# A decoder trunk on one core: the second rotary matmul of the attention scores on 128 rows where it took 64

## The chip, the cores and the metric

The kernel runs on one core of one Trainium2 chip. The metric is the device time of one execution in microseconds (us). Its engines run side by side and each takes its own instructions in order: TensorE (PE in the profile; PEld is its weight-load port), VectorE (DVE), ScalarE (ACT), GpSimd (POOL) and SyncE (SP), which issues the transfers. TensorE multiplies a stationary tile, loaded first, with a moving tile that streams through it; the sums collect in banks of PSUM.

## What is computed

The reference is a trunk of two layers on 512 tokens with 1024 channels: an HGRN2 recurrence in the first, latent attention (MLA) with 16 heads in the second, each with feed-forward half steps around it, and a gated embedding per layer. The change lies in the scores of the attention, which are the sum of a part without position (128 channels) and a rotary part (64 channels) whose key all heads share:

```python
s = (jnp.einsum('bqhd,bkhd->bhqk', qn, k_nope)
     + jnp.einsum('bqhd,bkd->bhqk', qr, k_rope)).astype(jnp.float32) * scale
...
s = jnp.where(mask[None, None], s, -jnp.inf)
pr = jax.nn.softmax(s, axis=-1).astype(v.dtype)
return jnp.einsum('bhqk,bkhd->bqhd', pr, v)
```

## The kernel before

Activations lie with channels on the 128 partitions and the 512 tokens along the row. Weights are one stream of 128x128 blocks in the order of use; a fetch brings eight of them (`raw`), ScalarE rounds them to a high half (`whi`, L125) and VectorE subtracts to get the low half (`wlo`, L126). Every float32 product is made of three matmuls on such halves: high by high, high by low and low by high (`mm3`, L142 to L144). `split` (L157, L158) makes the halves of an activation.

The instructions of an engine are put in order once, when the program is built, by a scheduler that works from the dependences and its own estimate of times. So TensorE's queue in the attention interleaves the scores of one head, the transposes and the weighting of the head before it, and the projections, and the order does not change at run time.

The attention is `mla`. For each head `scores` makes four blocks of 128 queries; block i has keys 0 to 128 (i + 1), so its matmuls stream 128, 256, 384 or 512 columns. A block takes five matmuls into one bank of the tag `aux`: the three of `mm3` for the channels without position, then two for the rotary part, L774 and L775. The tile `qr` of a head holds the 64 rotary channels twice: `rope` copies the high halves to partitions 0 to 63 and the low halves to 64 to 127. The key `krope` also holds its 64 channels twice, on partitions 0 to 63 and again on 64 to 127, because it comes out of a matmul with a constant that adds up pairs and repeats them; `krope[0]` is its high half and `krope[1]` its low half, both on 128 partitions.

L774 multiplies all 128 rows of `qr` with `krope[0]`: high by high and low by high at once. L775 multiplies rows 0 to 63 of `qr` with rows 0 to 63 of `krope[1]`: high by low. It ends the accumulation of the block. Behind it VectorE adds the mask and takes the maximum (L779, L783), ScalarE takes the exponential (L786), VectorE the reciprocal of the sum (L788) and GpSimd scales (L789). In `weigh` TensorE transposes the probabilities (L800), ScalarE and VectorE split them (`ph` L804, `pl` L805), and TensorE multiplies with the values.

In the first layer `recur` has other matmuls on a part of the array: at L440 it takes stationary tiles of 64 columns and writes 64 partitions.

Of the kernel before, what the change touches and what calls it, by code (L numbers as in the profile page):

```python
# [54 lines left out]
def kernel(  # L55
# [12 lines left out]
    act, dve, pool, pe = nc.scalar, nc.vector, nc.gpsimd, nc.tensor  # L68
# [14 lines left out]
    def slot(s="s", dt=F32, tag="s"):  # L83
        return spool.tile([P, T], dt, tag=tag, bufs=BUFS[tag], name=name(s))

    def tiny(n=4):
        return tpool.tile([P, n], F32, tag="t", bufs=40, name=name("t"))
# [4 lines left out]
    def aux_bank():  # L92
        return psum.tile([P, T], F32, tag="aux", bufs=4, name=name("aux"))
# [2 lines left out]
    FETCH_OFF = 200  # L96
    EV_OFF = 400

# [1 line left out]
    vc = cpool.tile([P, V_N], F32, name="vc")  # L100
    cs = cpool.tile([P, C_N], F32, name="cs")
    ident = cs[:, C_ID : C_ID + P]
# [3 lines left out]
    dve.memset(ones, 1.0)  # L106
    jmat = cs[:, C_J : C_J + P]

# [1 line left out]
    stream = {"n": 0, "tiles": 0, "ready": [], "now": None}  # L110

    def soon(n):
# [28 lines left out]
    def mm3(out, a, b, first, last):  # L141
        pe.matmul(out, a[0], b[0], start=first, stop=False)  # L142
        pe.matmul(out, a[0], b[1], start=False, stop=False)  # L143
        pe.matmul(out, a[1], b[0], start=False, stop=last)  # L144

    def chain(rhs):
        ps = mm_bank()
        n = len(rhs)
        for k in range(n):
            mm3(ps, block(), rhs[k], k == 0, k == n - 1)  # L150
        return ps

# [1 line left out]
    def split(src, scale=None, tag="s"):  # L154
        hi, lo = slot("hi", F32R, tag), slot("lo", F32R, tag)
        if scale is None:
            act.copy(hi, src)  # L157
            dve.tensor_tensor(out=lo, in0=src, in1=hi.bitcast(F32), op=ALU.subtract)  # L158
        else:
            act.activation(hi, src, AF.Copy, scale=scale)  # L160
            dve.scalar_tensor_tensor(  # L161
                out=lo, in0=src, scalar=scale, in1=hi.bitcast(F32), op0=ALU.mult, op1=ALU.subtract
            )
        return hi, lo

# [1 line left out]
    class Stats:  # L167
        def __init__(self, n):
            self.n, self.acc, self.seen = n, None, 0
# [50 lines left out]
        act.copy(rb, pb)  # L220
        return r, rb

# [1 line left out]
    x = [slot("x") for _ in range(KC)]  # L224

    def load(c):
# [2 lines left out]
    def gain(col, c):  # L229
        return vc[:, col + c : col + c + 1]  # L230

# [1 line left out]
    def ffn(xg, rb, post, beside=None, primed=()):  # L233
        primed = list(primed)
        for half in range(2):
            hidden = []
            for f in range(NH):
                pg, pu = (primed.pop(0) if primed else chain(xg) for _ in range(2))
                g = slot("g", F32, "r")
                dve.tensor_tensor(out=g, in0=pg, in1=rb, op=ALU.mult)  # L240
                act.activation(g, g, AF.Silu)  # L241
                pool.tensor_tensor(out=g, in0=g, in1=rb, op=ALU.mult)  # L242
                dve.tensor_tensor(out=g, in0=pu, in1=g, op=ALU.mult)  # L243
                hidden.append(split(g, None, "o" if f < 4 else "v" if f < 8 else "s"))
                if half == 1 and f == 5 and beside is not None:
                    beside()
            for m in range(KC):
                po = chain(hidden)
                dve.scalar_tensor_tensor(  # L249
                    out=x[m], in0=po, scalar=0.5, in1=x[m], op0=ALU.mult, op1=ALU.add  # L250
                )
                if half == 1:
                    post(m)
# [12 lines left out]
    def gcol(layer, i):  # L266
        return V_GAIN + (layer * 4 + i) * KC

# [1 line left out]
    def bounds():  # L270
        lbt = tpool.tile([P, 6 * A_HEADS], F32, tag="lb", bufs=1, name="lbt")
        lg0 = vc[:, V_LB : V_LB + A_HEADS]
        lg1 = vc[:, V_LB + A_HEADS : V_LB + 2 * A_HEADS]
        part = [lbt[:, i * A_HEADS : (i + 1) * A_HEADS] for i in range(6)]
        dve.tensor_tensor(out=part[0], in0=lg0, in1=lg1, op=ALU.max)
        dve.tensor_tensor(out=part[1], in0=lg0, in1=part[0], op=ALU.subtract)
        dve.tensor_tensor(out=part[2], in0=lg1, in1=part[0], op=ALU.subtract)
        act.activation(lbt[:, 3 * A_HEADS : 5 * A_HEADS], lbt[:, A_HEADS : 3 * A_HEADS], AF.Exp)
        dve.tensor_tensor(out=part[5], in0=part[3], in1=part[4], op=ALU.add)
        dve.reciprocal(part[0], part[5])  # L280
        dve.tensor_tensor(out=part[1], in0=part[3], in1=part[0], op=ALU.mult)
        dve.tensor_scalar(out=part[2], in0=part[1], scalar1=-1.0, scalar2=1.0, op0=ALU.mult, op1=ALU.add)
        return part[1], part[2]

# [1 line left out]
    def hgrn(xg, stats, lower, upper, post):  # L286
        rt, rb = rows(stats)
        mk = slot("mk", I32)
# [243 lines left out]
                    finish(2 * p + e, *res[e], sg[e])  # L532
        project(1)

# [1 line left out]
    def embed(layer):  # L536
        pp = []
        for c in range(2):
            raw = slot("p", F32, "r")
            nc.scalar.dma_start(raw, pT[layer, c * P : (c + 1) * P, :])  # L540
            pp.append(split(raw, None, "p"))
        return pp
# [15 lines left out]
            post(m)  # L558
        return emb

# [1 line left out]
    def last(xg, pp, rb):  # L562
        scaled, stats, halves = [], Stats(KC - 1), []

# [46 lines left out]
                        dve.tensor_tensor(out=o[:, c], in0=scaled[n][:, s], in1=r, op=ALU.mult)  # L611
                nc.sync.dma_start(view[i], o)

# [1 line left out]
    def rotary():  # L615
        pi_ = slot("pos", I32, "r")
        nc.scalar.dma_start(pi_, pos.to_broadcast([P, T]))
# [34 lines left out]
        act.activation(cos, rq, AF.Sin)  # L652
        return sin, cos

# [1 line left out]
    class Shared:  # L656
        def __init__(self):
            self.banks = [aux_bank() for _ in range(3)]
# [41 lines left out]
            cn.append(split(c))  # L700
        return cn, krope

# [1 line left out]
    def mla(xg, stats, cn, krope, sin, cos, post):  # L704
        _, rb = rows(stats)
        st = Stats(4)
# [33 lines left out]
        def values(p):  # L740
            w = [block(2) for _ in range(2)]
            tiles = []
            for i in range(2):
                pv = mm_bank()
                for n in range(2):
                    j = 2 * i + n
                    for k in range(2):
                        ck = tuple(a[:, j * P : (j + 1) * P] for a in cn[k])
                        mm3(pv[:, 256 * n : 256 * n + 256], ck, w[k], k == 0, k == 1)
                tiles.append(split(pv, None, "v"))  # L750
            return [
                [
                    tuple(a[:, 256 * (j % 2) + P * e : 256 * (j % 2) + P * e + P] for a in tiles[j // 2])
                    for j in range(NT)
                ]
                for e in range(2)
            ]

        def scores(qr):
            pk = chain(cn)  # L760
            kk = split(pk)
            pq = chain(cq)
            qq = split(pq)
            pt = [slot("P", F32, "r") for _ in range(3)]
            where = [(1, 384), (2, 0), (1, 0), (0, 0)]
            den = tiny()
            res = []
            for i in range(NT):
                w = (i + 1) * P
                qs = slice(i * P, w)  # L770
                ps = aux_bank()
                s = ps[:, 0:w]
                mm3(s, (qq[0][:, qs], qq[1][:, qs]), (kk[0][:, 0:w], kk[1][:, 0:w]), True, False)
                pe.matmul(s, qr[:, qs], krope[0][:, 0:w], start=False, stop=False)  # L774
                pe.matmul(s, qr[0:64, qs], krope[1][0:64, 0:w], start=False, stop=True)  # L775
                b, o = where[i]
                p = pt[b][:, o : o + w]
                mx, nb = tiny(1), tiny(1)
                dve.tensor_tensor_reduce(  # L779
                    out=p, in0=s, in1=cs[:, C_MASK + T - w : C_MASK + T], scale=1.0, scalar=-3.0e38,  # L780
                    op0=ALU.add, op1=ALU.max, accum_out=mx,
                )
                dve.tensor_scalar(  # L783
                    out=nb, in0=mx, scalar1=sc[:, i : i + 1], scalar2=-1.0, op0=ALU.mult, op1=ALU.mult
                )
                act.activation(p, p, AF.Exp, bias=nb, scale=sc[:, i : i + 1], accum_out=den[:, i : i + 1])  # L786
                rl = tiny(1)
                dve.reciprocal(rl, den[:, i : i + 1])  # L788
                pool.tensor_scalar(out=p, in0=p, scalar1=rl, scalar2=1.0, op0=ALU.mult, op1=ALU.mult)  # L789
                res.append(p)  # L790
            return res
# [34 lines left out]
        qr, vals = rope(0), values(0)  # L826
        last = None
        for h in range(B_HEADS):
            ahead = h < B_HEADS - 1
            rotated, value = qr[h % 4], vals[h % 2]  # L830
            if h % 4 == 3 and ahead:
                qr = rope(h // 4 + 1)
# [5 lines left out]
            last = (pr, value)  # L838
# [4 lines left out]
        for part in range(2):  # L843
            project(B_HEADS // 2 - 1, part)

# [1 line left out]
    first = Next([gcol(0, 0)])  # L847
    primed, heads = [mm_bank() for _ in range(4)], []

# [40 lines left out]
    tables, held = [], []  # L890
# [7 lines left out]
    sin, cos, lower, upper = tables  # L898
# [18 lines left out]
    cn, krope = shared(sh, sin, cos)  # L917
# [168 lines left out]
```

## Time and profile before

| | us |
|---|---|
| median of three runs | 2247.5 |
| lowest and highest run | 2247.43, 2249.44 |
| profiled execution: span, first to last instruction | 2245.4 |
| TensorE matmuls busy in the span | 2223.7 |
| VectorE busy | 1160.0 |
| ScalarE busy | 775.0 |
| GpSimd busy | 422.8 |

The profile gives the span of the profiled execution, and no other time of it. The matmuls of L775 start between 1513.3 and 1788.1 us of the span, all within the attention. In the timeline a row has the start, the time of the instruction, the engine, the line, the operation, what is written from what is read (the moving tile first, then the stationary one), the rows and columns of the array that are in use (128*128 is the whole array, 64*128 the upper half of its rows) and the moving tile's size. The time of a matmul overlaps with the next one's, so what a matmul takes of the queue is read from one start to the next.

### The profile page before, as it was taken

What the parts mean: (1) busy time and instruction counts of PE and PEld (TensorE: products, weight loads), DVE (VectorE), ACT (ScalarE), POOL (GpSimd) and SP (SyncE); (2) the same over time, 40 slices, a digit from 0 to 9 for tenths busy, and PEclk for the clock granted to TensorE, in tenths of its full rate; (3) what the DMA queues carried; (4) which work ended last, traced back from release to release, by engine and by line L of the source; (5) the groups of instructions that cost most, each with busy time, mean ns of one, the idle gap of its engine ahead of it and who ended that gap; (6) DMA issues with size and microseconds to landing.
All of it is one profiled execution on the core that took longest, in us unless ns stands there. A gap on an engine that the chain in (4) does not pass through costs nothing.

```text
span 2245.4 us, 26413 instructions
## 1 busy us (share of the span) xinstructions
PE 2223.7 (99%) x10434; PEld 1847.4 (82%) x10434; DVE 1160.0 (52%) x1798; ACT 775.0 (35%) x1125; POOL 422.8 (19%) x441
## 2 busy tenths in 40 slices
PE   8999999999999999999999999999999999999998
PEld 6888888899888888888888888887878788888887
DVE  5433544778875433445654344466666664334345
ACT  4322333223343222334432132345444442223244
POOL 2100111555431101111111011112111121001111
PEclk9999999999999999999999999999999999999999
DMA  4333332222223333332333333332223123333332
GB/s 163 98 94 98 104 94 90 83 67 66 67 66 103 96 101 94 105 102 89 99 94 94 103 95 94 101 95 77 62 71 94 38 85 94 97 101 103 99 99 66
DMA packets 60523, 204.42 MB, mean 91 GB/s; under 512 B 7408, under 2 KB 9584, under 8 KB 60400
## 3 DMA queue, kind: packets, MB, share of 16 engines
q1 hardware_dynamic: 59536, 201.28, 29.3%
q8 instruction: 82, 1.34, 0.3%
q10 hardware_dynamic: 864, 1.46, 0.2%
q14 instruction: 41, 0.34, 0.0%
HBM read 196.42 MB, written 2.10 MB: 88 GB/s over the span
## 4 chain that ended last, share of the span: by engine, by line
PE 98%; DVE 1%; ACT 0%; issue 0%; DMA 0%; POOL 0%; SPq 0%; DVEq 0%; ACTq 0%
PE mm L142 29%; PE mm L143 29%; PE mm L144 29%; PE aux L144 1%; PE aux L143 1%; PE aux L396 1%; PE aux L142 1%; PE aux L775 1%; PE aux L800 1%; PE aux L774 0%; PE aux L205 0%; PE aux L213 0%; PE aux L196 0%; PE aux L440 0%; DVE o L611 0%
## 5 line engine op out<-in xcount | busy, mean ns | idle before, releaser
L142 PE MATMUL mm<-hi,whi 128*128 128x512 f32 x2824 | 1097.2, 391 | 8.5 <-ACT whi L125 6.2
L143 PE MATMUL mm<-lo,whi 128*128 128x512 f32 x2824 | 1103.6, 391 | 2.0 <-DVE lo L161 2.0
L144 PE MATMUL mm<-hi,wlo 128*128 128x512 f32 x2824 | 1101.0, 390 | 0.0
L125 ACT CAST whi<-raw 128x1024 fp32r<-128x1024 f32 (+2 forms) x372 | 386.5, 1041 | 1101.0 <-PE mm L143 792.0
L142 PEld LDWEIGHTS mm<-hi,whi 128*128 128x128 f32 x2824 | 530.1, 188 | 119.8 <-ACT whi L125 6.2
L143 PEld LDWEIGHTS mm<-lo,whi 128*128 128x128 f32 x2824 | 530.8, 188 | 111.5 <-DVE lo L161 4.1
L144 PEld LDWEIGHTS mm<-hi,wlo 128*128 128x128 f32 x2824 | 530.8, 188 | 110.0 <-issue 0.9
L126 DVE TENSOR_TENSOR wlo<-raw,whi 128x1024 fp32r<-128x1024 f32 (+2 forms) x372 | 463.9, 1248 | 273.2 <-ACT whi L125 253.5
L242 POOL TENSOR_TENSOR g<-g,rb 128x512 f32<-128x512 f32 x88 | 152.0, 1729 | 984.3 <-ACT g L241 984.3
L243 DVE TENSOR_TENSOR g<-mm,g 128x512 f32<-128x512 f32 x88 | 60.9, 691 | 262.7 <-PE mm L144 254.1
L240 DVE TENSOR_TENSOR g<-mm,rb 128x512 f32<-128x512 f32 x88 | 60.4, 691 | 205.9 <-PE mm L144 205.9
L179 POOL TENSOR_TENSOR sq<-sq,sq 128x512 f32<-128x512 f32 x55 | 80.6, 1465 | 334.9 <-ACT sq L174 334.1
L249 DVE SCALAR_TENSOR_TENSOR x<-mm,x 128x512 f32<-128x512 f32 x64 | 44.2, 691 | 106.7 <-PE mm L144 105.6
L789 POOL TENSOR_SCALAR P<-P,t 128x128 f32<-128x128 f32 (+1 forms) x64 | 35.3, 551 | 243.7 <-DVE t L788 207.3
L160 ACT ACTIVATE hi<-x,vc 128x512 fp32r<-128x512 f32 x72 | 51.4, 718 | 77.4 <-DVE x L249 57.3
L161 DVE SCALAR_TENSOR_TENSOR lo<-x,vc,hi 128x512 fp32r<-128x512 f32 x72 | 63.1, 884 | 25.5 <-ACT hi L160 25.4
L158 DVE TENSOR_TENSOR lo<-g,hi 128x512 fp32r<-128x512 f32 x88 | 60.1, 685 | 0.9 <-ACT hi L157 0.7
L786 ACT ACTIVATE P<-P,t,t 128x128 f32<-128x128 f32 (+1 forms) x64 | 42.0, 656 | 53.6 <-DVE t L783 53.3
L822 DVE TENSOR_TENSOR x<-mm,x 128x512 f32<-128x512 f32 x64 | 43.7, 687 | 26.0 <-PE mm L144 25.6
L157 ACT CAST hi<-g 128x512 fp32r<-128x512 f32 x88 | 54.5, 621 | 6.8 <-DVE g L243 6.8
L241 ACT ACTIVATE g<-g 128x512 f32<-128x512 f32 x88 | 55.0, 628 | 1.8 <-DVE g L240 1.2
L142 PE MATMUL mm<-whi,hi 128*128 128x256 f32 x192 | 55.2, 288 | 0.0
(199 smaller groups left out, 1596.6 us busy)
## 6 DMA issues: line engine op xcount, KB each, us to landing
raw<-in_wall SPq DMA_DIRECT2D x367, 512.0 KB, 3.5
x<-in_xT SPq DMA_DIRECT2D x8, 256.0 KB, 5.8
qr<-hi SPq DMA_DIRECT2D x32, 64.0 KB, 2.0
qr<-lo SPq DMA_DIRECT2D x32, 64.0 KB, 2.0
out_dram<-o SPq DMA_DIRECT2D x8, 256.0 KB, 2.5
p<-in_pT ACTq DMA_DIRECT2D x4, 256.0 KB, 2.8
cs<-in_cst SPq DMA_DIRECT2D x1, 385.0 KB, 7.2
pos<-in_pos ACTq DMA_DIRECT2D x1, 256.0 KB, 3.2
```

The lines of the kernel that those rows point to most:

```text
L125: act.copy(hi[:, s], raw[:, s])
L126: dve.tensor_tensor(out=lo[:, s], in0=raw[:, s], in1=hi[:, s].bitcast(F32), op=ALU.subtract)
L142: pe.matmul(out, a[0], b[0], start=first, stop=False)
L143: pe.matmul(out, a[0], b[1], start=False, stop=False)
L144: pe.matmul(out, a[1], b[0], start=False, stop=last)
L158: dve.tensor_tensor(out=lo, in0=src, in1=hi.bitcast(F32), op=ALU.subtract)
L161: dve.scalar_tensor_tensor(out=lo, in0=src, scalar=scale, in1=hi.bitcast(F32), op0=ALU.mult, op1=ALU.subtract)
L179: eng.tensor_tensor(out=self.acc, in0=self.acc, in1=sq, op=ALU.add)
L240: dve.tensor_tensor(out=g, in0=pg, in1=rb, op=ALU.mult)
L241: act.activation(g, g, AF.Silu)
L242: pool.tensor_tensor(out=g, in0=g, in1=rb, op=ALU.mult)
L243: dve.tensor_tensor(out=g, in0=pu, in1=g, op=ALU.mult)
```

## The change

The second rotary matmul takes all 128 partitions of both operands. It thereby adds the product of the low halves of queries and keys, which lie on partitions 64 to 127, to the same sum. The number of instructions, their order on all five engines, their buffers and their waits are the same; in the program the size of the array's part at L775 is 128 by 128 where it was 64 by 128. Elsewhere the diff only takes comments out.

```diff
@@ scores, in mla @@
                 mm3(s, (qq[0][:, qs], qq[1][:, qs]), (kk[0][:, 0:w], kk[1][:, 0:w]), True, False)
                 pe.matmul(s, qr[:, qs], krope[0][:, 0:w], start=False, stop=False)
-                pe.matmul(s, qr[0:64, qs], krope[1][0:64, 0:w], start=False, stop=True)
+                pe.matmul(s, qr[:, qs], krope[1][:, 0:w], start=False, stop=True)
```

## Rows read from the trace of the kernel before

**Rows 1.** The page: the span, and the chain that ended last by engine.

```profile
span 2245.4 us, 26413 instructions
...
PE 98%; DVE 1%; ACT 0%; issue 0%; DMA 0%; POOL 0%; SPq 0%; DVEq 0%; ACTq 0%
```

**Rows 2.** Windows, attention stretch: its length, busy us of each engine (instructions), clock.

```profile
1510.00:1790.00 280.00, 277.88 (x1396) 222.31 (x1395) 184.79 (x450) 132.53 (x266) 42.61 (x69) 1.00 0.24 71
```

**Rows 3.** Both rotary lines: weight loads, min/median/max ns, first and last start.

```profile
L774 PEld LDWEIGHTS aux<-hi,qr x64: 186/188/192, 1513.0 to 1787.6; 128*128 128x128 f32 x64
...
L775 PEld LDWEIGHTS aux<-lo,qr x64: 182/183/183, 1513.3 to 1788.1; 64*128 64x128 f32 x64
```

**Rows 4.** Timeline of TensorE's matmuls around one block of 512 columns.

```profile
1526.14 0.39 PE L142 MATMUL aux<-hi,hi 128*128 128x512 f32 x1
...
1526.59 0.39 PE L144 MATMUL aux<-hi,lo 128*128 128x512 f32 x1
1526.82 0.39 PE L774 MATMUL aux<-hi,qr 128*128 128x512 f32 x1
1527.13 0.50 PE L775 MATMUL aux<-lo,qr 64*128 64x512 f32 x1
1527.56 0.50 PE L144 MATMUL mm<-hi,wlo 128*128 128x512 f32 x1
1527.90 0.39 PE L142 MATMUL mm<-hi,whi 128*128 128x512 f32 x1
```

**Rows 5.** Timeline of the load port there; in brackets the idle time before.

```profile
1527.13 0.18 PEld L775 LDWEIGHTS aux<-lo,qr 64*128 64x128 f32 x1 [0.35 <-issue]
1527.56 0.19 PEld L144 LDWEIGHTS mm<-hi,wlo 128*128 128x128 f32 x1 [0.25 <-issue]
```

**Rows 6.** Timeline of TensorE's matmuls, one head's blocks of 128, 256, 384 columns.

```profile
1536.27 0.27 PE L144 MATMUL aux<-ph,lo 128*128 128x128 f32 x1
1536.38 0.28 PE L774 MATMUL aux<-hi,qr 128*128 128x128 f32 x1
...
1536.83 0.38 PE L142 MATMUL aux<-hi,hi 128*128 128x256 f32 x1
1537.06 0.28 PE L143 MATMUL aux<-lo,hi 128*128 128x256 f32 x1
...
1537.29 0.28 PE L774 MATMUL aux<-hi,qr 128*128 128x256 f32 x1
...
1537.81 0.44 PE L142 MATMUL aux<-hi,hi 128*128 128x384 f32 x1
1538.09 0.34 PE L143 MATMUL aux<-lo,hi 128*128 128x384 f32 x1
...
1538.44 0.34 PE L774 MATMUL aux<-hi,qr 128*128 128x384 f32 x1
...
1539.08 0.50 PE L143 MATMUL mm<-lo,whi 128*128 128x512 f32 x1
1539.42 0.40 PE L144 MATMUL mm<-hi,wlo 128*128 128x512 f32 x1
```

**Rows 7.** Timeline around two groups of L440, first layer: exit, then entry.

```profile
435.81 0.50 PE L144 MATMUL mm<-hi,wlo 128*128 128x512 f32 x1
436.15 0.39 PE L142 MATMUL mm<-hi,whi 128*128 128x512 f32 x1
...
440.71 0.39 PE L144 MATMUL mm<-hi,wlo 128*128 128x512 f32 x1
441.03 0.68 PE L440 MATMUL aux<-qq,k 128*64 128x64 f32 x8
```

**Rows 8.** Waits of TensorE's matmuls in 1510 to 1790: us, times, longest.

```profile
PE aux L143 <- DVE pl L805: 1.1, 3, 0.5
PE aux L144 <- DVE lo L158: 0.5, 1, 0.5
PE aux L142 <- ACT ph L804: 0.2, 1, 0.2
```

## Prediction

> **What bounds the kernel now.** I read the views from the outside in. First the page: the chain of work that ended last is TensorE's own for 98% of a span of 2245.4 us [rows 1], so a microsecond taken out of TensorE's queue is a microsecond of the kernel unless a wait takes its place. Then the windows view of the stretch in which all 64 executions of the changed line fall, 1510 to 1790 us [rows 2]: TensorE's matmuls are busy 277.88 of 280.00 us there, VectorE 184.79, ScalarE 132.53, and the granted clock is 1.00, the upper of its two levels (2.4 GHz). TensorE is the bound of this stretch with much room beside it. Busy time does not tell what a matmul costs, though, because matmuls overlap; the cost is the distance from one start to the next. So the third view is the timeline of TensorE around the changed line (L775), and the reader should subtract neighbouring starts.
>
> **The steady pitch.** Between full-array matmuls of the same width the starts lie 0.227 us apart at 512 columns (three steps from 1526.14 to 1526.82 cover 0.68) [rows 4], 0.175 at 384 (two steps from 1538.09 to 1538.44), 0.12 at 256 (two steps from 1537.06 to 1537.29, 0.115 before rounding up) and 0.11 at 128 (1536.27 to 1536.38) [rows 6]. The full-array first rotary matmul (L774) sits in this pitch: it starts one pitch behind its predecessor.
>
> **What the half-array matmul costs today.** In the same block L775 starts 0.31 us behind L774, not 0.227; the matmul behind it starts 0.43 later (1527.13 to 1527.56), and the one after that 0.34 later (1527.56 to 1527.90) [rows 4]. Only then is the pitch back. The weight loads show why: L775's load begins after 0.35 us in which the load port waited for nothing that the profile shows, and the next full-array load again after 0.25 us [rows 5]. Both loads begin at the very time at which their own matmul is put down as started (1527.13 and 1527.56 in both views) [rows 4, 5], so no matmul ahead hides them: neither on the way into the half array nor on the way out. The cost is therefore not in the 64 rows but in two changes of the array's shape.
>
> A second place in the trace agrees, with another shape: the 64-column matmuls of the first layer (L440, 128*64). Going in, the first one starts 0.32 us behind a 512-wide full-array matmul (440.71 to 441.03); coming out, the second full-array matmul starts 0.34 us behind the first (435.81 to 436.15) [rows 7]. These are the same two numbers, 0.31 and 0.34, at a place that shares neither tile nor line with the attention. What the two places share is the change of shape.
>
> **What the change removes.** It adds no instruction and moves none: on all five engines the order is the same. L774, just ahead, already reads all 128 rows of the same query tile, so no transfer is waited for that was not waited for before. The 64 matmuls of L775 (one for each of the 64 loads of [rows 3]) become what L774 is: the same stationary tile, a moving tile of the same kind and width. I cost each at one pitch of its width and let the two shape changes go. From the start of L774, over three steps (L774, L775, the one behind), I take today's distance less three pitches:
> - 512 columns: 1526.82 to 1527.90 is 1.08 us, less 3 x 0.227 = 0.68, leaves 0.40 [rows 4].
> - 384 columns, followed by 512: 1538.44 to 1539.42 is 0.98, less 0.175 + 0.175 + 0.227 = 0.58, leaves 0.40 [rows 6].
> - 256 columns, followed by 384: 1537.29 to 1538.09 is 0.80, less 0.12 + 0.12 + 0.175 = 0.415, leaves 0.385 [rows 6].
> - 128 columns, followed by 256: 1536.38 to 1537.06 is 0.68, less 0.11 + 0.11 + 0.12 = 0.34, leaves 0.34 [rows 6].
>
> One head has one of each: 0.40 + 0.40 + 0.385 + 0.34 = 1.525 us. There are 16 heads, and the blocks that follow each other directly share no step, so nothing is counted twice: 16 x 1.525 = 24.4 us. The rows allow some 0.2 us more or less (rounding of hundredths). The upper end is about 1.3 us higher: a wide load behind a narrow full-array matmul can be hidden partly in the work ahead, and 16 such places at up to 0.08 us (0.11 less 0.03, if the narrow matmul cost next to nothing) give that. So 25.7 us is the most.
>
> **What can be given back.** TensorE arrives earlier at each wait behind the scores. The waits that it has in this stretch are few: 1.1 us in three places for the low half of the probabilities (L805), 0.5 in one for a low half (L158), 0.2 in one for a high half (L804) [rows 8]. At each of these five places the wait could grow by what TensorE has gained since the last one. If that is a whole head's gain each time, 5 x 1.525 = 7.6 us are lost; that is the lower end, a gain of 16.8. If nothing is lost, zero. I take 1 us, close to zero, because the chain that is waited for at the L805 and L804 places starts with the transposes of the probabilities on TensorE itself, behind the scores: it starts earlier by as much as its reader does. What is not started by TensorE, the splitting of weights, runs on engines that are idle for 95 us (VectorE) and 147 us (ScalarE) of the 280 [rows 2]; shortening the stretch by 24 us leaves both well below TensorE.
>
> **Sum.** 24.4 less 1.0 is 23.4 us. Against the profiled execution: 2245.4 - 23.4 = 2222.0 us of span. The median of the runs, 2247.5, stands 2.1 us above that span; I carry these over: 2224.1 us, a ratio of 0.990.
>
> **Rivals.**
> *The rows do not matter (same time).* The mechanism: a matmul and its load take what their columns take, and the excess around L775 belongs to something that stays, such as the end of the accumulation in that bank or the same query tile being loaded twice. The result is 2247.5 us. For it: the loads are as long, 183 ns at 64 rows and 188 at 128 [rows 3]. Against it: the last matmul of an accumulation in another bank (L144 at 1536.27, the end of the weighting) has its successor one pitch behind [rows 6], and L440 pays it with neither property [rows 7]. The Trainium skill states the rule in "TensorE: Matmul & The Clock Gate", section "LDWEIGHTS (loading the stationary operand)": a load with fewer rows takes the same time, since columns alone count; by that rule alone the time would stay at 2247.5. The same skill in "TensorEngine Tiling (Array Packing)", section "Key Properties", says that a change of tiling mode, unlike a change of tile, drains the engine. The trace agrees with both: equal loads, but not hidden at a change of shape. I give this rival 0.05.
>
> *Only one side goes, or the waits take much of it.* If the excess behind L775 stayed (0.20 + 0.11 of each 0.40) and only the 0.09 ahead of it went, 64 x 0.09 = 5.8 us would be gained: 2241.7. If on the other hand all of it went but waits took two thirds back, it would be near 2239. Between 6 and 16.8 us of gain I put 0.06. For it speak the three places at which TensorE already waits for L805 [rows 8].
>
> *The half array is the cheaper one (slower).* The mechanism: a matmul on 64 rows leaves half of the array free, so it overlaps with its neighbours, and filling the array takes that away. The place is the two steps around L775; the price, if it had been wholly free, is one pitch of each width: 16 x (0.227 + 0.175 + 0.12 + 0.11) = 10.1 us, 2257.6 us. It decides once the two steps from L774 to the matmul behind L775 are shorter than two pitches today; they are 0.74 us (1526.82 to 1527.56) against 0.45 [rows 4]. I give it 0.02.
>
> **How the numbers follow.** The forecast (a gain of 16.8 to 25.7 us) has 0.87, the partial gain 0.06, no change 0.05, slower 0.02. The predicted time is the forecast's, 2224.1. Its range runs from 2247.5 - 25.7 = 2221.8 to 2247.5 - 16.8 = 2230.7; with a few tenths for the spread of the runs below, 2221 to 2231. This holds 0.87 by itself, so no rival has to be taken in. About 0.2% (4.5 us) is what a measurement of this kernel tells from no change; the forecast and the partial gain lie beyond it: faster 0.93, same 0.05, slower 0.02.
>
> **What would show it.** In the trace of the changed kernel L775 should start one pitch behind L774 (0.23 us at 512 columns), the matmul behind it one pitch later, and the 0.35 and 0.25 us of load-port idle [rows 5] should be gone, with a clock still at 1.00. The five waits of [rows 8] should add up to less than 3 us. Starts at 0.31 and 0.43 us apart as now would prove the first rival; starts in the steady pitch with a gain under 17 us would mean that waits for L805, L804 or L158 have grown, and their rows would say by how much.

## The result, and the profile after

The changed kernel takes 2223.98 us (median; 2223.92 to 2224.34) where the one before takes 2247.47 in the same comparison: a ratio of 0.9893, with a 95% interval of 0.9879 to 0.9907. That is 23.5 us less; 2224.1 was predicted. The profiled execution has a span of 2222.2 us against 2245.4 [rows 1].

From the page of the changed kernel, the span and the chain by engine; then the windows view of the attention (length, then busy us of matmuls, loads, VectorE, ScalarE and GpSimd with their instructions, clock, share of the transfer engines, GB/s):

```profile
span 2222.2 us, 26413 instructions
...
PE 96%; DVE 2%; ACT 1%; issue 0%; DMA 0%; POOL 0%; SPq 0%; DVEq 0%; ACTq 0%
```

```profile
1510.00:1766.60 256.60, 254.50 (x1396) 220.11 (x1395) 182.95 (x446) 131.13 (x264) 42.33 (x68) 1.00 0.26 77
```

The same 1396 matmuls that filled 280.00 us [rows 2] now fill 256.60, with the clock at 1.00 as before. The stretch is 23.4 us shorter and the span 23.2, so the whole difference lies here. Read from the start of L774 over three steps, the 64 blocks together take 33.4 us where they took 56.8, which is the same 23.4. VectorE and ScalarE are busy nearly as long in the stretch (182.95 and 131.13 us against 184.79 and 132.53, about 1% less), so their shares rise, but TensorE is still the one that is full: it is idle for 2.1 us, as before.

The chain passes through TensorE for 96% of the span where it was 98 [rows 1]. From about 1513.5 to 1542 us it now runs through VectorE, ScalarE and a transfer, and it comes back to TensorE at a wait of 0.2 us for L805 (1542.05). The wait at the same place was 0.2 us before, too, but there the chain stayed on TensorE up to the transposes just ahead of it.

The next two views answer [rows 4] and [rows 5]: the timeline of TensorE's matmuls around the same block of 512 columns, and that of its load port. The columns are start, time of the instruction, engine, line, operation, written from read, the part of the array in use, and the moving tile.

```profile
1524.59 0.39 PE L774 MATMUL aux<-hi,qr 128*128 128x512 f32 x1
1524.81 0.39 PE L775 MATMUL aux<-lo,qr 128*128 128x512 f32 x1
1525.04 0.39 PE L144 MATMUL mm<-hi,wlo 128*128 128x512 f32 x1
1525.27 0.39 PE L142 MATMUL mm<-hi,whi 128*128 128x512 f32 x1
```

```profile
1524.59 0.19 PEld L775 LDWEIGHTS aux<-lo,qr 128*128 128x128 f32 x1
1524.82 0.19 PEld L144 LDWEIGHTS mm<-hi,wlo 128*128 128x128 f32 x1
```

L775 starts 0.22 us behind L774, and the two matmuls behind it 0.23 apart, where the distances were 0.31, 0.43 and 0.34. The load of L775 now begins at 1524.59, with the matmul of L774, and the one behind it at 1524.82, with L775's own; both idle marks are gone. The loads themselves are not shorter: the median of L775's is 188 ns where it was 183 [rows 3].

The narrower blocks of one head, the rows that answer to [rows 6]:

```profile
1533.74 0.28 PE L774 MATMUL aux<-hi,qr 128*128 128x128 f32 x1
1533.86 0.28 PE L775 MATMUL aux<-lo,qr 128*128 128x128 f32 x1
1533.97 0.33 PE L142 MATMUL aux<-hi,hi 128*128 128x256 f32 x1
1534.14 0.28 PE L143 MATMUL aux<-lo,hi 128*128 128x256 f32 x1
...
1534.38 0.28 PE L774 MATMUL aux<-hi,qr 128*128 128x256 f32 x1
...
1534.61 0.34 PE L142 MATMUL aux<-hi,hi 128*128 128x384 f32 x1
1534.79 0.34 PE L143 MATMUL aux<-lo,hi 128*128 128x384 f32 x1
...
1535.14 0.33 PE L774 MATMUL aux<-hi,qr 128*128 128x384 f32 x1
...
1535.48 0.39 PE L143 MATMUL mm<-lo,whi 128*128 128x512 f32 x1
1535.71 0.40 PE L144 MATMUL mm<-hi,wlo 128*128 128x512 f32 x1
```

Over the three steps from L774, 384 columns take 0.57 us (0.98 before), 256 take 0.41 (0.80) and 128 take 0.40 (0.68); 512 columns, above, take 0.68 (1.08). A head gains 0.41 + 0.39 + 0.28 + 0.40 = 1.48 us, and 16 like it 23.7; over all 16 heads as they are it is the 23.4 above.

The waits of TensorE's matmuls in the stretch (us, times, longest), the rows that answer to [rows 8], have not changed:

```profile
PE aux L143 <- DVE pl L805: 1.1, 3, 0.5
PE aux L144 <- DVE lo L158: 0.5, 1, 0.5
PE aux L142 <- ACT ph L804: 0.2, 1, 0.2
```

### The profile page after: what moved, and what is told of

The parts are those of the page before. It is cut to its first block, busy times and chain, and to the rows that moved or that the text cites. A ratio compares the mean times of both kernels' runs of the same rounds, so it can differ in the third digit from the quotient of the medians.

```text
span 2222.2 us, 26413 instructions
## 1 busy us (share of the span) xinstructions
PE 2200.4 (99%) x10434; PEld 1845.4 (83%) x10434; DVE 1158.4 (52%) x1798; ACT 774.4 (35%) x1125; POOL 423.3 (19%) x441
## 4 chain that ended last, share of the span: by engine, by line
PE 96%; DVE 2%; ACT 1%; issue 0%; DMA 0%; POOL 0%; SPq 0%; DVEq 0%; ACTq 0%
PE mm L142 29%; PE mm L143 29%; PE mm L144 29%; PE aux L396 1%; PE aux L143 1%; PE aux L144 1%; PE aux L142 1%; PE aux L800 1%; PE aux L774 0%; PE aux L775 0%; PE aux L205 0%; PE aux L213 0%; DVE wlo L126 0%; PE aux L196 0%; DVE lo L158 0%
## 5 line engine op out<-in xcount | busy, mean ns | idle before, releaser
L143 PE MATMUL mm<-wlo,hi 128*128 128x256 f32 x192 | 55.0, 287 | 0.0
```

## The experiments

The theory: what L775 cost beyond its columns was two changes of the array's shape in each block, in and out, in which a weight load can't begin under the matmul ahead of it. Its rivals: the cost goes with rows that are not in use; each half-array matmul costs more by itself, whatever stands beside it; the excess belongs to the end of an accumulation, or to the query tile being loaded twice in a row.

### Rows out of use without a change of shape

```diff
-                pe.matmul(s, qr[:, qs], krope[1][:, 0:w], start=False, stop=True)
+                pe.matmul(s, qr[0:96, qs], krope[1][0:96, 0:w], start=False, stop=True)
```

> L775 takes rows 0 to 95 of both operands, where the kernel before takes 64 and the changed one 128 (a third of the low-by-low channels is left in, two thirds are left out). The program gives it the whole array as its part, so no change of shape stands around it, but only 96 rows are in use. If the cost was the change of the array's shape, the time is the changed kernel's, 2224 us within 2, and L775 stands in the steady pitch (0.23 us at 512 columns). If it is the number of rows in use that costs, anything under 128 rows pays: 2247 us within 2, with 0.31 and 0.43 us around L775, or about half way, 2236, if it goes in proportion to the missing rows.

Measured: 2224.98 us, 0.9897 of the kernel before (0.9883 to 0.9912). The timeline of TensorE's matmuls at the same block:

```profile
1525.97 0.39 PE L774 MATMUL aux<-hi,qr 128*128 128x512 f32 x1
1526.19 0.40 PE L775 MATMUL aux<-lo,qr 96*128 96x512 f32 x1
1526.43 0.40 PE L144 MATMUL mm<-hi,wlo 128*128 128x512 f32 x1
1526.66 0.40 PE L142 MATMUL mm<-hi,whi 128*128 128x512 f32 x1
```

L775 has 96 rows in use and stands in the steady pitch: 0.22, 0.24 and 0.23 us. The median is 1.0 us above that of the changed kernel and the lowest run 0.2 us above its lowest (2224.11 and 2223.92), so a quarter of the rows idle costs at most some 1 us of the 23.5: it is not the idle rows that cost. What sets this run apart from the kernel before is the part of the array that the program gives the instruction, 128 by 128 here and 64 by 128 there; the part is read from the program, the trace shows only the rows in use. No number of rows between 64 and 96 was run.

### Two half-array matmuls in a row

```diff
-                pe.matmul(s, qr[0:64, qs], krope[1][0:64, 0:w], start=False, stop=True)
+                for z in range(2):
+                    pe.matmul(s, qr[0:64, qs], krope[1][0:64, 0:w], start=False, stop=z == 1)
```

> The kernel before with L775 issued twice in a row on 64 rows, so its product is counted twice; 64 more matmuls, but as many changes of shape as before, 64 in and 64 out. If the change of shape costs, the second of each pair adds one pitch: 16 x (0.227 + 0.175 + 0.12 + 0.11) = 10.1 us, 2257.6 us within 3, and the two starts of a 512-column pair are 0.23 us apart. If each half-array matmul costs by itself, the second adds its excess as well: 10.1 + 24.4 = 34.5 us, 2282 us. If half-array matmuls overlapped with each other, it would add less than 10.

Measured: 2256.27 us, a ratio of 1.0037 (1.0024 to 1.005). That is 8.7 us more than the kernel before, for 64 more matmuls. The timeline of the matmuls around a block of 512 columns, where both rows of the pair are merged (x2) and the line is L776 in this kernel; the same from a window that leaves out the first of the pair; and the load port:

```profile
1528.84 0.39 PE L774 MATMUL aux<-hi,qr 128*128 128x512 f32 x1
1529.15 0.73 PE L776 MATMUL aux<-lo,qr 64*128 64x512 f32 x2
```

```profile
1529.49 0.39 PE L776 MATMUL aux<-lo,qr 64*128 64x512 f32 x1
1529.81 0.50 PE L142 MATMUL mm<-hi,whi 128*128 128x512 f32 x1
1530.15 0.40 PE L143 MATMUL mm<-lo,whi 128*128 128x512 f32 x1
```

```profile
1529.15 0.30 PEld L776 LDWEIGHTS aux<-lo,qr 64*128 64x128 f32 x2 [0.35 <-issue]
1529.81 0.19 PEld L142 LDWEIGHTS mm<-hi,whi 128*128 128x128 f32 x1 [0.36 <-issue]
```

The pair is entered after 0.31 us, as the single one was, and the full matmul starts 0.66 us behind the pair's first: 0.43, as behind the single one, and one pitch of 0.23. There is one idle mark for the two loads, not two. In sum the second half-array matmul, with a neighbour of its own shape, costs its columns and no more.

One expectation was missed: the two starts of the pair are not 0.23 us apart but 0.34 (1529.15 to 1529.49). The full matmul then starts 0.32 behind the second, and the one after it 0.34 later (1529.81 to 1530.15). So at 512 columns the way in and the way out cost alike: the matmul behind a change of shape starts 0.09 us late, and the one behind that another 0.11. Around a single half-array matmul the 0.11 of the way in and the 0.09 of the way out fall on the same distance: 0.227 + 0.11 + 0.09 = 0.43.

### The same pair on the whole array

```diff
-                pe.matmul(s, qr[:, qs], krope[1][:, 0:w], start=False, stop=True)
+                for z in range(2):
+                    pe.matmul(s, qr[:, qs], krope[1][:, 0:w], start=False, stop=z == 1)
```

> The changed kernel with L775 issued twice in a row on 128 rows (its product is counted twice); TensorE's order is the same as in the run with two half-array matmuls, so the two differ in the rows of L775 alone. If the change of shape costs, this run is 24 us within 2 below that one, as the changed kernel is below the one before: 2234 us within 3. If each half-array matmul costs by itself, the difference is twice that, 48 us.

Measured: 2232.6 us, a ratio of 0.9931 (0.9917 to 0.9946). The pair of a block of 512 columns and the matmul behind it:

```profile
1524.93 0.61 PE L776 MATMUL aux<-lo,qr 128*128 128x512 f32 x2
1525.39 0.39 PE L142 MATMUL mm<-hi,whi 128*128 128x512 f32 x1
```

The difference between the two pairs is 2256.27 - 2232.6 = 23.7 us, with TensorE's order the same in both. It is the difference that one half-array matmul per block makes (23.5), and not twice that. So the excess is counted per block, not per matmul. The rival of a cost of each matmul by itself falls here. Both pairs add some 8.7 us where one pitch each had been put at 10.1. The second matmul itself is not cheaper than its pitch (the two above take 0.46 us, two pitches). But adding a matmul also makes the scheduler order the rest of the attention anew, and the other 1.4 us must lie there; where is open. So these two runs are compared with each other rather than with the single ones. An overlap of half-array matmuls, which was expected to show as less than 10 us, is not the reason, as the pair on the whole array adds no more.

### The half-array matmul first in the block

```diff
-                mm3(s, (qq[0][:, qs], qq[1][:, qs]), (kk[0][:, 0:w], kk[1][:, 0:w]), True, False)
-                pe.matmul(s, qr[:, qs], krope[0][:, 0:w], start=False, stop=False)
-                pe.matmul(s, qr[0:64, qs], krope[1][0:64, 0:w], start=False, stop=True)
+                pe.matmul(s, qr[0:64, qs], krope[1][0:64, 0:w], start=True, stop=False)
+                mm3(s, (qq[0][:, qs], qq[1][:, qs]), (kk[0][:, 0:w], kk[1][:, 0:w]), False, False)
+                pe.matmul(s, qr[:, qs], krope[0][:, 0:w], start=False, stop=True)
```

> The kernel before with the half-array matmul as the first of the five of a block instead of the last; L774 ends the accumulation. The scheduler puts some of the half-array matmuls side by side, so that 54 changes of shape each way are left of 64. If the change of shape costs, about 0.38 x 10 = 3.8 us of 24.4 are gained: 2243.7 us, within 3 as the rest of TensorE's order differs a little. If the excess belongs to the end of an accumulation or to the query tile being loaded twice in a row, it is gone: 2223 us. If each half-array matmul costs by itself, nothing is gained: 2247.5 us.

Measured: 2243.04 us, a ratio of 0.9981 (0.9971 to 0.9991); eight of the ten runs lie within 0.3 us of this median, the other two at 2244.39 and 2247.46. That is 4.5 us gained for 10 changes of shape each way that are gone of 64. The timeline of this kernel's matmuls at two places (L773 is the half-array matmul, L775 now the full one that ends the block):

```profile
1509.98 0.39 PE L144 MATMUL mm<-hi,wlo 128*128 128x512 f32 x1
1510.29 0.91 PE L773 MATMUL aux<-lo,qr 64*128 64x128 f32 x4
1511.13 0.92 PE L142 MATMUL aux<-hi,hi 128*128 128x128 f32 x4
...
1514.94 0.39 PE L775 MATMUL aux<-hi,qr 128*128 128x512 f32 x1
1515.17 0.40 PE L142 MATMUL mm<-hi,whi 128*128 128x512 f32 x1
...
1518.59 0.39 PE L142 MATMUL mm<-hi,whi 128*128 128x512 f32 x1
1518.91 0.32 PE L773 MATMUL aux<-lo,qr 64*128 64x128 f32 x1
1519.16 0.33 PE L142 MATMUL aux<-hi,hi 128*128 128x128 f32 x1
```

At 1518.91 the half-array matmul opens the accumulation, follows a matmul that loads another tile, and still starts 0.32 us behind it; the next starts 0.25 later, as behind a 128-column L775 before (1536.58 to 1536.83 in the trace of before). L775, which now ends the accumulation, has its successor one pitch behind (1514.94 to 1515.17). The end of an accumulation and the repeated tile are thus ruled out as the cause. At 1510.29 four half-array matmuls stand in a row: they are entered once, after 0.31 us, and left once.

### Another shape: the 64-column matmuls of the first layer

```diff
                 pe.matmul(
-                    sc[0:64, j * 64 : (j + 1) * 64],
-                    k[:, j * P : j * P + 64],
+                    sc[:, j * 64 : (j + 1) * 64],
+                    k[:, j * P : (j + 1) * P],
                     q[:, j * P + 64 : (j + 1) * P],
```

The edit is made on the changed kernel, so that no change of shape is left in the program; the changed kernel ran beside it as the measure.

> The changed kernel, with L440 of the first layer on the whole array too: the stationary tile has 128 columns where it had 64, and the lower half of what it writes is not read. The output is the same. There are 7 stretches of L440 with a change of shape on either side. If any change of shape costs, the 0.32 us on the way in and the 0.34 us behind the way out become a steady pitch, 7 x about 0.35 = 2.4 us. But each of the 64 loads then has 128 columns, and its pitch goes from 0.058 to 0.11 us: 64 x 0.05 = 3.3 us. The sum is 0.9 us slower than the changed kernel, 2224.9 us within 2; the scheduler also moves neighbours of L440 in TensorE's order. If only the row shape costs and not the column shape, the 0.32 and 0.34 us stay and the time is 2227 us.

> The changed kernel once more, as the measure for the run beside it: 2224.0 us within 1, by every theory.

Measured: 2225.18 us, and 2224.24 for the changed kernel alone: 0.94 us slower. The timelines of TensorE's matmuls at one group, first of the changed kernel, then of this one:

```profile
500.32 0.39 PE L144 MATMUL mm<-hi,wlo 128*128 128x512 f32 x1
500.64 1.15 PE L440 MATMUL aux<-qq,k 128*64 128x64 f32 x16
501.71 0.50 PE L142 MATMUL mm<-hi,whi 128*128 128x512 f32 x1
502.05 0.39 PE L143 MATMUL mm<-lo,whi 128*128 128x512 f32 x1
```

```profile
498.22 0.39 PE L144 MATMUL mm<-hi,wlo 128*128 128x512 f32 x1
498.45 1.00 PE L440 MATMUL aux<-qq,k 128*128 128x64 f32 x8
499.28 0.44 PE L454 MATMUL aux<-qq,k 128*128 128x128 f32 x2
```

The 0.32 us on the way in is now a pitch of 0.23. The 0.34 us on the way out, which was expected to go as well, nearly stays. Where a 512-column matmul follows the group directly in this kernel, the matmul behind it still starts 0.32 us later (436.34 to 436.66), with the whole array throughout:

```profile
435.53 1.00 PE L440 MATMUL aux<-qq,k 128*128 128x64 f32 x8
436.34 0.48 PE L144 MATMUL mm<-hi,wlo 128*128 128x512 f32 x1
436.66 0.40 PE L142 MATMUL mm<-hi,whi 128*128 128x512 f32 x1
```

So the 0.34 us behind the L440 groups can't be put down to the change of shape: a wide matmul behind narrow ones shows nearly the same without any. The attention of the changed kernel has it too: behind four transposes of 128 columns (L800), a 512-column matmul has its successor 0.32 us behind (1526.53 to 1526.85). What does become shorter on the way out is the step before, from the last matmul of the group to the wide one: 0.15 us in the changed kernel (501.56 to 501.71), 0.08 in this one.

Eight matmuls take 0.83 us to the next start (498.45 to 499.28), where sixteen took 1.07 (500.64 to 501.71): 0.10 each against 0.07. Their loads, 64 in all, take 192 ns (median) where they took 138. The 0.94 us agrees with the sum that was made beforehand (0.9), but its two terms don't: less came back than the 0.35 us for each group (0.09 on the way in, 0.07 and 0.02 on the way out), and the pitch rose by 0.03 to 0.04 us instead of 0.05. The spread of the runs (2224.94 to 2225.47) and the order that the scheduler changed around L440 are of the size of the difference, too. What this run shows stands in its timeline; its time proves neither term.

## Why the prediction was right

*The bound.* TensorE's queue set the time, and what was taken out of it came off the kernel: 23.4 us over the 64 blocks, 23.2 in the span, 23.5 in the median.

*The two changes of shape.* This step was argued from the start distances and from L440; the runs show it for the attention. Idle rows alone cost next to nothing (96 rows), a second half-array matmul costs its columns alone, four in a row are entered and left once, and neither the accumulation's end nor the repeated tile carries the excess. Of the second place, L440, the way in bears it out (0.32 us with the change of shape, 0.23 without). The 0.34 on the way out [rows 7] was misread: it is still 0.32 without a change of shape, and what the change of shape costs there is 0.07 us one step earlier. Nor does L440 lack both properties of the first rival, as the prediction says: each of its matmuls ends an accumulation of its own (`stop=True`). The Trainium skill says in "TensorEngine Tiling (Array Packing)", section "Key Properties", that a change of tiling mode drains the engine; the traces agree for rows and for columns (0.31 and 0.32 us on the way in, where the pitch is 0.23). How the array empties is not seen in a trace; what is seen is that the load doesn't begin under the matmul ahead.

*The terms.* 512, 384 and 256 columns came out as put: 0.40, 0.41 and 0.39 us in the head shown against 0.40, 0.40 and 0.385. The term of 128 columns was too large: 0.28 against 0.34. The step behind L775 was put at 0.11 and is 0.11, but the one after it, from the first 256-column matmul to the second, takes 0.17 (1533.97 to 1534.14), where I had put 0.12. Behind the narrow matmuls the loads come 0.11 us apart (1533.80, 1533.91, 1534.02), so the load of the second wide one begins 0.05 us behind the start of the matmul ahead of it, where in the steady pitch it begins with that start. So 0.05 us of the old 0.23 were never due to the change of shape; over 16 heads that is 0.8 us. Averaged over all heads the terms are 0.395, 0.393, 0.386 and 0.288 us. The 1.3 us that I added to the gain as its upper end, for work behind a narrow matmul that would be hidden better, is shown by no run: in no block of 128 columns is a step from L774 or L775 under 0.109 us, and the wide matmul behind it has its successor later, not earlier.

*What was given back.* I took 1.0 us for grown waits, and there was none: the three rows of waits are the same to a tenth before and after. The reason that I gave for a small loss was that the chain which is waited for begins on TensorE behind the scores. It does not hold at every place: at 1542.05 the L805 that is waited for now stands behind other work in VectorE's own queue, and the wait is as short as before all the same (0.2 us). Of the 24.4 us some 1 us was thus missing in the blocks (23.4), nearly all of it in the 128-column term, and none in the waits. The sum was right to 0.1 us because one error stood where the other had been expected. That is luck; the size of the two terms was known less well than the result makes it look.

*The rivals.* That rows do not matter was right for the load's own time (183 and 188 ns) and, in the run with 96 rows, for the kernel; wrong was that the excess belongs to something that stays. The partial gain would have needed an excess that stayed behind L775, or longer waits; beyond the 0.05 us of the narrow blocks there was neither. Its split of the 0.40 us, 0.09 ahead of L775 and 0.31 behind it, is not the split between way in and way out: by the pair of 512 columns each of them costs 0.09 + 0.11 = 0.20 us. That the half array were the cheaper one is excluded by the pairs as well: with neighbours of the same shape the second matmul adds some 8.7 us on half the array as on the whole.

## What to carry to other kernels

Look for matmuls on a part of the array that stand alone among full ones. The marks are a start distance above the pitch of the width, and idle time of the load port ahead of the load that the profile puts down to no other engine (`issue`; here 32 of the 64 loads have it). A late successor alone is no mark: a wide matmul behind narrow ones shows it as well. If the missing rows can be filled without a wider stationary tile, with a product that is welcome anyway (or, not tried here, with zeros), fill them; if not, put the partial ones side by side. Price it from starts, and against the wider load: here each lone block cost 0.3 to 0.4 us, and filling up the 64-column matmuls brought nothing.

## What was not expected of the hardware

A matmul on 96 rows takes the whole array's part and pays next to nothing, while one on 64 rows pays 0.4 us in a 512-column block: fewer rows in use are slower here only where the program gives the instruction a smaller part of the array. And a wide matmul behind a narrow one has its successor late even without any change of shape: 0.17 us at 256 columns behind 128, where the pitch is 0.12, and 0.32 at 512 columns, where it is 0.23.
